# A written-out instruction order, priced anew, and one store moved to another queue, in a hybrid encoder block

## The chip, the core and the metric

The kernel runs on one core of a Trainium2 chip. A core has five engines with an instruction stream each: PE (TensorE, the matmuls, with PEld as its weight load), DVE (VectorE), ACT (ScalarE), POOL (GpSimd) and SP (SyncE, here only an issuer of DMAs). The metric is the device time of one execution in microseconds; less is better. The kernel before was timed in three runs.

## What is computed

One layer with width 1024 over 2048 tokens, in float32:

```python
hn = rmsnorm(h, mix_norm_g)
u, g_ssm, q, k, v, g_attn = split(hn @ w_in)            # six times 512 columns
y_ssm = s5_branch(u, ...) * silu(g_ssm)                 # diagonal complex state space, GELU, GLU
y_att = stick_breaking_branch(q, k, v, ...) * silu(g_attn)   # 8 heads of 64, strictly causal
h = h + concat(y_ssm, y_att) @ w_out
h = h + sigmoid(rmsnorm(h) @ w_ple_gate) * (p @ w_ple_proj)
...
# stick-breaking, for each block of 128 queries:
z = q @ k.T / 8
later = reverse_cumsum(log_sigmoid(-z)) - log_sigmoid(-z)
weights = exp(log_sigmoid(z) + later)                   # strictly below the diagonal
out = weights @ v
```

## The kernel before, in words

**Stages.** The work goes through five stages, which overlap.

1. `phase_u` (L547): eight units T of 256 tokens. `load_x` (L551) loads x, normalizes it, transposes it on PE in 64-row pieces (L527), splits it into a rounded part and a rest (`split`, L512) and stores it for later (hn, L565). Then u is projected with three matmuls for each product (L542 to L544: high by high, high by rest, rest by high). ACT copies the four results into the tile `uq` (L589), and at each odd T a DMA stores `uq` into the DRAM scratch tensor u, 1 MB at a time: four DMAs (L592), issued by POOL.
2. `ssm_chain` (L171) makes the state space's tables on DVE, beside stage 1.
3. `ssm_pack`, `ssm_batch` and `gate_unit`, eight batches of four state-space groups. Each batch loads its u for all tokens (`us`, L387), so the first needs all four stores of u. Matmuls L358, L364, L407, L467 to L470 and scans on DVE; POOL takes some products. `gate_unit` (L596) projects the gate.
4. Attention. Head pairs hp = 0 to 3, each with 16 blocks of 128 queries; block i of pair hp stands in step t = i + 8 hp, so up to two pairs run side by side. `attn_proj` (L662) projects q, k, v and the gate (L657 to L659, 128x512, three matmuls for each product; transposes L690, L691). `attn_block` (L701) goes through the keys in chunks of up to 512. For each chunk and both heads: z on PE, two heads abreast on 64 rows each (L718, six matmuls); ACT makes two sigmoids, px (L723) and be (L728); POOL masks the diagonal (L732); DVE runs a reverse scan of px (L734); POOL multiplies be by it (L736); PE transposes the weights in 64-row pieces, two abreast (L527, into ps_wt); ACT or DVE copies them out (L745, L743). For every two chunks the products with v follow (L753, two heads abreast on 64 columns each). The GLU of the state-space branch (`glu_unit`, L634) is mixed into the last eight steps.
5. `phase_out` (L829): 16 blocks of 128 rows, w_out (L657 to L659 into ps_h) and the gated embedding (into ps_p and ps_g).

**PSUM.** Eight banks are named z0, z1, w0, w1, tr, ssm, acc and o. z and the weights' transposes use two each for one chunk (z0 and z1, w0 and w1).

**Tilings.** PE uses the whole array for projections, half the rows for z and the 64-row transposes, and half the columns for the products with v. In the planner these are the modes "all", "rows" and "cols".

**What sets the order.** The order within each engine is not the order of the program text. When the program is written, `arrange` (L1293) lays out one order for each engine and adds it as dependencies. `plan` (L1077) lists for each instruction what it must wait for, its engine, and a length from `duration` (L1049), with the mode of each matmul. `list_schedule` (L1188) then runs a model: at each step it takes the engine that is free first and gives it the ready instruction of the best rank. Instructions ready are kept apart by mode; one of the present mode may be taken although another's rank is better by up to `near` (4 us); a change of mode costs a flat `change` (0.2 us). A DMA holds the modelled link for its bytes at 290 GB/s, behind 1.5 us and ahead of 2 us. `best_order` (L1260) does this six times, forward and then backward over reversed dependencies; the backward times give the next forward ranks, and the order with the earliest modelled end is kept. Groups written inside `abreast` (the pairs on half arrays) stay together.

An order, once laid out, is fixed: an engine whose next instruction has to wait does not take a later one. SP issues its DMAs in such an order too.

Of the kernel before, what the change touches and what calls it, by code (L numbers as in the profile page):

```python
# [18 lines left out]
P = 128  # L19
# [527 lines left out]
def phase_u(e, pool, xp, chain):  # L547
# [26 lines left out]
    for T in range(NT // 2):  # L574
        if 2 <= T + 1 < NT // 2:
            xts[T + 1] = load_x(T + 1)
        xt = xts.pop(T - 2, None)
        xt = xts[T]
        if T % 2 == 0:
            uq = pool.tile([P, L, 4, NCH // 4], F32, tag="uq", name="uq", bufs=2)  # L580
        ps = [e.bank("ps_u", "w0", "w1", "o", "acc")[:, :256] for _ in range(4)]
        if T == 2:
            e.mark()
        for ct, c in [(ct, c) for c in range(NC8) for ct in range(4)] if T == 0 else [(ct, c) for ct in range(4) for c in range(NC8)]:
            cs = slice(ct * P, (ct + 1) * P)
            mm3(e, ps[ct], (w[c][:, 0, cs], w[c][:, 1, cs]), (xt[:, :, 0, c], xt[:, :, 1, c]), c == 0, c == NC8 - 1)
        for ct in range(4):
            k0 = (T % 2) * (NCH // 8)
            nc.scalar.activation(uq[:, :, ct, k0:k0 + NCH // 8], ps[ct].rearrange("p (c j) -> p j c", j=L), AF.Copy)  # L589
        if T % 2 == 1:  # L590
            c0 = (T // 2) * (NCH // 4)
            nc.gpsimd.dma_start(e.u_d[:, :, c0:c0 + NCH // 4].rearrange("j (k p) c -> p (j k) c", p=P), uq.rearrange("p j k c -> p (j k) c"))  # L592
    return prep, xts


# [453 lines left out]
def duration(i, name, outs, ins, psum):  # L1049

    n = max([a[1] for a in outs + ins] or [1])
    eng = str(i.engine).split(".")[-1]
    if name == "InstDMACopy":
        return (0.6 if eng == "Pool" else 0.45), 0.0
    if name == "InstMatmult":
        cols, kind = outs[0][1], ins[0][2]
        if i.is_transpose:
            return (0.031 if ins[0][0] <= 64 else 0.109), 0.12
        if "float32r" in kind or "bfloat16" in kind:
            return {512: 0.228, 256: 0.120}.get(cols, max(cols / 2255.0, 0.058)) / (2 if ins[0][0] <= 64 else 1), 0.12  # L1060
        half = min(outs[0][0], ins[0][0]) <= 64
        return (1 if half else 2) * max(cols / 1160.0, 0.056), 0.12
    if eng == "Activation":
        return 0.193 + n * 0.00082, 0.0
    if eng == "Pool":
        if name == "InstTensorTensor" and "pow" in str(i.op).lower():
            return 0.45 + 0.15 * n, 0.0
        base, slope = {"InstMemset": (0.1, 0.0008), "InstTensorCopy": (0.5, 0.001), "InstTensorScalarPtr": (0.3, 0.001), "InstTensorScalarAffineSelect": (0.35, 0.0008)}.get(name, (0.47, 0.00175))
        return base + slope * n, 0.0
    if name == "InstTensorScalarPtr" and i.is_tensor_tensor_scan:  # L1070
        return 0.22 + n * 0.0027, 0.0
    if name in ("InstMemset", "InstTensorCopy") and not psum:
        return 0.11 + n * 0.0006, 0.0
    return 0.15 + n * 0.00107, 0.0


def plan(tc, pools):  # L1077
# [27 lines left out]
    for k, i in enumerate(mybir_i):  # L1105
# [79 lines left out]
    return _seen[key]  # L1185


def list_schedule(ops, pre, soft, length, mode, rank, near=4.0, change=0.2):  # L1188

    import heapq  # L1190
    n = len(ops)
# [3 lines left out]
    for k in range(n):  # L1195
        for q in (*pre[k], *soft[k]):
            after[q].append(k)
    for e in set(eng):
        free[e], wait[e], ready[e], order[e], now[e] = 0.0, [], {}, [], None

# [9 lines left out]
    for k in range(n):  # L1210
        if not open_[k]:
            heapq.heappush(wait[eng[k]], (0.0, rank[k], k))
    for _ in range(n):
        best = None
        for e in free:
            while wait[e] and wait[e][0][0] <= free[e]:
                _, r, k = heapq.heappop(wait[e])
                heapq.heappush(ready[e].setdefault(mode.get(k), []), (r, k))
            if any(ready[e].values()):
                c = (free[e], 0, e)  # L1220
            elif wait[e]:
# [6 lines left out]
        if late:  # L1228
            k = heapq.heappop(wait[e])[2]
        else:  # L1230
            m = min((h for h in ready[e] if ready[e][h]), key=lambda h: ready[e][h][0][0] - near * (h == now[e]))
            k = heapq.heappop(ready[e][m])[1]
        t = max(t, due(k))
        if now[e] != mode.get(k):
            t += change
            now[e] = mode.get(k)
        start[k] = t
        free[e] = t + length[k][0]
        if length[k][2]:
            link = max(t + 1.5, link) + length[k][2] / 290e3  # L1240
            done[k] = link + 2.0
# [18 lines left out]
def best_order(ops, pre, soft, length, mode, rows, turns=6):  # L1260
# [23 lines left out]
    for _ in range(turns):  # L1284
        order, start, done = list_schedule(ops, pre, soft, length, mode, lead([k - 1e5 if k in soon else r for k, r in enumerate(rank)], first))
        if best is None or max(done) < best[0]:
            best = max(done), order, start
        _, _, done = list_schedule(ops, back, loose, length, mode, lead([-t for t in done], last))
        rank = [-t for t in done]
    return best  # L1290

# [37 lines left out]
```

## Time and profile before

| What | us |
|---|---|
| median of three runs (1605.31 to 1606.29) | 1605.36 |
| profiled execution | 1606.73 |
| its span, first to last instruction | 1604.8 |
| PEld busy | 1254.5 |
| DVE busy | 1079.1 |
| ACT busy | 825.2 |
| POOL busy | 766.3 |

The difference between span and execution is 1.9 us around the instructions. Instruction counts and busy shares stand in the page's first part. The three matmuls of attn_proj are the largest group on PE, with 480 instructions to a line. The page's groups name the line, the engine, what is written from what, shapes, count, busy time, the mean of one in ns, and the idle time ahead of them with what ended it. The chain of waits follows the work that ended last back to the start. The table of windows gives each engine's busy time in a stretch of the span. The timeline gives starts and durations in order. A matmul's duration runs to its modelled end, and successive matmuls overlap: for the rate at which PE goes on, one looks at the difference of two starts.

### The profile page before, as it was taken

To read this page: it belongs to the slowest core of one execution; us is meant where nothing else is said; L and a number is where in the kernel's file an instruction comes from. 1 tells how busy PE (TensorE), PEld (TensorE's weight loads), DVE (VectorE), ACT (ScalarE), POOL (GpSimd) and SP (SyncE) were. 2 spreads that over 40 slices of the span, in tenths; PEclk is the share of its full clock that TensorE was granted. 3 is DMA by queue.
4 is the path that set the end of the run, shared out by engine and by line. 5 is a ranking of instruction groups with operands and counts; after the bars stand their busy time and mean duration, and the time that the engine had idled before them with its cause. 6 is when DMAs were issued, how large, how long until landed. Compare 5 with 4: busy or idle time off the path is not lost.

```text
span 1604.8 us, 31108 instructions
## 1 busy us (share of the span) xinstructions
PE 1548.5 (96%) x11878; PEld 1254.5 (78%) x11878; DVE 1079.1 (67%) x1980; ACT 825.2 (51%) x1850; POOL 766.3 (48%) x882
## 2 busy tenths in 40 slices
PE   6999898999999999999999999999989999999998
PEld 6998888987777777777777776777678788888887
DVE  6895948868678997789987899748764432332322
ACT  6643435456566776677766777646544221121211
POOL 2242434437578898688967798747630000000000
PEclk9999999999999999999999999999999999999999
DMA  9897535455332323323233234432354221212210
GB/s 294 262 289 194 175 118 181 156 174 193 113 113 84 112 91 132 113 85 108 95 132 112 86 109 112 109 96 68 107 164 126 83 79 50 86 60 69 64 49 33
DMA packets 147670, 195.58 MB, mean 122 GB/s; under 512 B 63697, under 2 KB 110753, under 8 KB 136129
## 3 DMA queue, kind: packets, MB, share of 16 engines
q1 hardware_dynamic: 145552, 186.45, 36.1%
q0 software_dynamic: 1968, 7.15, 2.2%
q8 instruction: 94, 1.54, 0.4%
q14 instruction: 56, 0.45, 0.1%
HBM read 145.44 MB, written 48.12 MB: 121 GB/s over the span
## 4 chain that ended last, share of the span: by engine, by line
PE 79%; DVE 11%; issue 4%; POOL 3%; ACT 1%; DMA 1%; SPq 0%; POOLq 0%; DVEq 0%; ACTq 0%
PE ps_qk L657 7%; PE ps_qk L659 7%; PE ps_qk L658 7%; PE ps_o L753 6%; PE ps_z L718 5%; PE ps_wt L527 4%; PE ps_g L659 4%; PE ps_h L657 4%; PE ps_h L658 4%; PE ps_g L658 4%; PE ps_h L659 4%; PE ps_g L657 4%; DVE px L734 3%; POOL be L736 2%; PE ps_u L543 2%
## 5 line engine op out<-in xcount | busy, mean ns | idle before, releaser
L736 POOL TENSOR_TENSOR be<-be,px 128x512 f32<-128x512 f32 (+3 forms) x320 | 404.1, 1275 | 136.6 <-DVE px L734 51.0
L734 DVE TENSOR_TENSOR_SCAN px<-px 128x512 f32<-128x512 f32 (+3 forms) x320 | 424.6, 1338 | 52.6 <-ACT px L723 37.0
L723 ACT ACTIVATE px<-ps_z 128x512 f32<-128x512 f32 (+3 forms) x320 | 170.0, 539 | 78.8 <-PE ps_z L718 51.9
L657 PE MATMUL ps_qk<-w_w,xt 128*128 128x512 f32 x480 | 198.7, 414 | 1.2 <-DVE gn L60 1.2
L658 PE MATMUL ps_qk<-w_w,xt 128*128 128x512 f32 x480 | 195.4, 407 | 0.0
L659 PE MATMUL ps_qk<-w_w,xt 128*128 128x512 f32 x480 | 195.3, 407 | 0.0
L508 POOL TENSOR_TENSOR rs_h<-rs_h,mhalf 128x1 f32<-128x1 f32 x16 | 9.1, 572 | 381.8 <-DVE rs_h L67 381.8
L728 ACT ACTIVATE be<-ps_z 128x512 f32<-128x512 f32 (+3 forms) x320 | 170.4, 545 | 5.4 <-PE ps_wt L527 5.4
L745 ACT ACTIVATE ws<-ps_wt 128x512 f32<-128x512 f32 (+3 forms) x256 | 129.0, 540 | 79.3 <-PE ps_wt L527 78.5
L718 PE MATMUL ps_z<-k,q 64*128 64x512 f32 (+3 forms) x960 | 138.5, 392 | 2.4 <-ACT be L728 1.5
L753 PE MATMUL ps_o<-ws,v 128*64 128x128 f32 x2176 | 138.3, 278 | 0.0
L753 PEld LDWEIGHTS ps_o<-ws,v 128*64 128x64 f32 x2176 | 118.7, 138 | 22.2 <-issue 18.1
L527 PEld LDWEIGHTS ps_wt<-ident,be 64*128 64x128 f32 x2176 | 83.1, 138 | 51.6 <-issue 25.6
L657 PEld LDWEIGHTS ps_qk<-w_w,xt 128*128 128x128 f32 x480 | 90.2, 188 | 32.1 <-issue 11.9
L659 PEld LDWEIGHTS ps_qk<-w_w,xt 128*128 128x128 f32 x480 | 90.3, 188 | 24.2 <-issue 5.7
L658 PEld LDWEIGHTS ps_qk<-w_w,xt 128*128 128x128 f32 x480 | 90.5, 189 | 23.5 <-issue 5.8
L527 PE MATMUL ps_wt<-ident,be 64*128 64x64 f32 x2176 | 102.9, 229 | 5.8 <-POOL be L736 2.8
L514 ACT ACTIVATE yr<-yt 128x512 fp32r<-128x512 f32 x32 | 20.2, 632 | 162.7 <-PE ps_h L659 157.3
L657 PE MATMUL ps_h<-w_w,yr 128*128 128x512 f32 x256 | 100.7, 393 | 2.3 <-ACT yr L514 2.3
L659 PE MATMUL ps_g<-w_wg,hr 128*128 128x512 f32 x256 | 101.5, 397 | 0.0
L658 PE MATMUL ps_g<-w_wg,hr 128*128 128x512 f32 x256 | 101.1, 395 | 0.0
L658 PE MATMUL ps_h<-w_w,yr 128*128 128x512 f32 x256 | 100.6, 393 | 0.0
(378 smaller groups left out, 3608.5 us busy)
## 6 DMA issues: line engine op xcount, KB each, us to landing
xt<-hn SPq DMA_DIRECT2D x60, 1024.0 KB, 4.9
hn<-xt SPq DMA_DIRECT2D x16, 1024.0 KB, 9.5
wst<-in_w_in_dram SPq DMA_DIRECT2D x48, 256.0 KB, 5.3
xg<-hn SPq DMA_DIRECT2D x12, 1024.0 KB, 7.0
x<-in_x_dram SPq DMA_DIRECT2D x16, 512.0 KB, 7.0
out_dram<-o SPq DMA_DIRECT2D x32, 256.0 KB, 2.0
h<-in_x_dram SPq DMA_DIRECT2D x15, 512.0 KB, 4.3
u<-uq POOLq DMA_DIRECT2D x4, 1024.0 KB, 18.3
```

The lines of the kernel that those rows point to most:

```text
L527: e.nc.tensor.transpose(ps[h][:, 64 * k:64 * k + 64], v[r], e.ident[r, r])
L543: mm(out, wh, xl, start=False, stop=False)
L657: mm(out, xh, wh, start=first, stop=False)
L658: mm(out, xh, wl, start=False, stop=False)
L659: mm(out, xl, wh, start=False, stop=last)
L718: nc.tensor.matmul(z[:, :n], q[half[h], a], A.k[ch][half[h], b, :n], start=s == 0, stop=s == 2)
L723: nc.scalar.activation(px[:, :n], z[:, :n], AF.Sigmoid, scale=-(HD ** -0.5))
L728: nc.scalar.activation(be[:, :n], z[:, :n], AF.Sigmoid, scale=HD ** -0.5)
L734: nc.vector.tensor_tensor_scan(rv, rv, rv, initial=1.0 if carry[h] is None else carry[h], op0=ALU.mult, op1=ALU.bypass)
L736: nc.gpsimd.tensor_tensor(be[:, :n], be[:, :n], px[:, 1:n + 1], op=ALU.mult)
L745: nc.scalar.activation(dst, ps, AF.Copy)
L753: nc.tensor.matmul(po[half[h], :P], A.v[sb][:, h], w[:, h, b], start=sb == i, stop=sb == 0)
```

## The change

One line of the kernel's own work is touched: the four stores of u are issued by SP and not by POOL. The rest is in the planner:

- `duration`: a DMA issued by POOL takes 0.6 us plus 0.27 ns for each piece (contiguous run of elements, counted by the new `pieces`). POOL's general instructions have base 0.2 us and not 0.47, its diagonal masks 0.25 and not 0.35; DVE's scan is 0.2 + 0.002 n and not 0.22 + 0.0027 n (n elements a partition).
- `plan`: on the link a piece counts for at least 220 bytes. DVE and POOL instructions that touch no PSUM get the mode "shared". The 64-row transposes get the mode "turn", which stands with "rows" when ready instructions are chosen, and apart from it when a change is priced.
- `list_schedule`: `near` is 8 us. A change costs what the new function `change` says, by the mode left and the one entered. With `stay` = 0.3 us: where the choice would leave the present mode, and an instruction of the present mode will be ready within 0.3 us with a rank at most `near` behind, the engine idles until then. A "shared" instruction that begins while the other engine of DVE and POOL is in one is lengthened by 0.45 of the overlap, or of its own length plus 0.2 us if that is less. In backward passes the change is priced with the two modes exchanged.

```diff
-            nc.gpsimd.dma_start(e.u_d[:, :, c0:c0 + NCH // 4].rearrange("j (k p) c -> p (j k) c", p=P), uq.rearrange("p j k c -> p (j k) c"))
+            nc.sync.dma_start(e.u_d[:, :, c0:c0 + NCH // 4].rearrange("j (k p) c -> p (j k) c", p=P), uq.rearrange("p j k c -> p (j k) c"))
...
-        return (0.6 if eng == "Pool" else 0.45), 0.0
+        return (0.6 + pieces(i) * 0.00027 if eng == "Pool" else 0.45), 0.0
...
-        base, slope = {"InstMemset": (0.1, 0.0008), "InstTensorCopy": (0.5, 0.001), "InstTensorScalarPtr": (0.3, 0.001), "InstTensorScalarAffineSelect": (0.35, 0.0008)}.get(name, (0.47, 0.00175))
+        base, slope = {"InstMemset": (0.1, 0.0008), "InstTensorCopy": (0.5, 0.001), "InstTensorScalarPtr": (0.3, 0.001), "InstTensorScalarAffineSelect": (0.25, 0.0008)}.get(name, (0.2, 0.00175))
...
-        return 0.22 + n * 0.0027, 0.0
+        return 0.2 + n * 0.002, 0.0
...
-        length.append(duration(i, type(i).__name__, outs, ins, psum) + ((outs[0][0] * outs[0][1] * 4 if type(i).__name__ == "InstDMACopy" else 0),))
+        length.append(duration(i, type(i).__name__, outs, ins, psum) + ((max(outs[0][0] * outs[0][1] * 4, pieces(i) * 220) if type(i).__name__ == "InstDMACopy" else 0),))
+        if not psum and str(i.engine).split(".")[-1] in ("DVE", "Pool") and type(i).__name__ not in ("InstDMACopy", "InstRegisterMove"):
+            mode[k] = "shared"
         if type(i).__name__ == "InstMatmult":
-            mode[k] = "rows" if ins[0][0] <= 64 else "cols" if outs[0][0] <= 64 else "all"
+            mode[k] = ("turn" if i.is_transpose else "rows") if ins[0][0] <= 64 else "cols" if outs[0][0] <= 64 else "all"
...
-def list_schedule(ops, pre, soft, length, mode, rank, near=4.0, change=0.2):
+def change(a, b):
+
+    if a == b or a is None or b is None or (a, b) == ("turn", "rows"):
+        return 0.0
+    if (a, b) == ("rows", "turn"):
+        return 0.09
+    return {"rows": 0.19, "turn": 0.12, "cols": 0.148, "all": 0.097}[a] + (0.1 if b == "all" else 0.0)
+
+
+def list_schedule(ops, pre, soft, length, mode, rank, near=8.0, stay=0.3, back=False):
...
             m = min((h for h in ready[e] if ready[e][h]), key=lambda h: ready[e][h][0][0] - near * (h == now[e]))
+            if m != now[e] and now[e] is not None:
+                r = ready[e][m][0][0]
+                soon = [w[0] for w in wait[e] if w[0] <= free[e] + stay and tiling.get(w[2]) == now[e] and w[1] - near <= r]
+                if soon:
+                    free[e] = min(soon)
+                    continue
...
-        if now[e] != mode.get(k):
-            t += change
-            now[e] = mode.get(k)
+        if k in tiling:
+            t += change(mode[k], last[e]) if back else change(last[e], mode[k])
+        now[e], last[e] = tiling.get(k), mode.get(k)
+        held = length[k][0]
+        if mode.get(k) == last.get(peer.get(e)) == "shared":
+            held += 0.45 * min(held + 0.2, max(0.0, free[peer[e]] - t))
...
-        free[e] = t + length[k][0]
+        free[e] = t + held
```

More of the change, by code (lines that the diff above doesn't have):

```diff
@@ L1074, in duration, with pieces @@
     return 0.15 + n * 0.00107, 0.0
+def pieces(i):
+    runs, total = [], 1
+    for side in (i.ins, i.outs):
+        run, total = 1, 1
+        ap = [(int(s), int(c)) for s, c in side[0].ap]
+        for s, c in reversed(ap):
+            if s == run:
+                run *= c
+            elif c > 1:
+                break
+        for _, c in ap:
+            total *= c
+        runs.append(run)
+    return total // min(runs)
 def plan(tc, pools):
@@ L1212, in list_schedule @@
             heapq.heappush(wait[eng[k]], (0.0, rank[k], k))
-    for _ in range(n):
+    left = n
+    while left:
         best = None
@@ L1217, in list_schedule @@
                 _, r, k = heapq.heappop(wait[e])
[L1218 removed]
+                heapq.heappush(ready[e].setdefault(tiling.get(k), []), (r, k))
             if any(ready[e].values()):
```

5 lines of the change are left out of this document (4 added, 1 removed).

## The prediction

> **What bounds the kernel now.** I read the page first: the busy shares, then the chain that ended last.
>
> ```profile
> span 1604.8 us, 31108 instructions
> PE 1548.5 (96%) x11878; PEld 1254.5 (78%) x11878; DVE 1079.1 (67%) x1980; ACT 825.2 (51%) x1850; POOL 766.3 (48%) x882
> PE 79%; DVE 11%; issue 4%; POOL 3%; ACT 1%; DMA 1%; SPq 0%; POOLq 0%; DVEq 0%; ACTq 0%
> ```
>
> TensorE is busy 96% of the span and holds 79% of the chain. A plan cannot change how many matmuls there are, so it can win time in two ways only: by leaving PE fewer idle stretches, or by making what counts as busy denser. The table by stretches says where either is to be had. Its columns are the stretch, its length, then busy time of PE, PEld, DVE, ACT, POOL, the granted clock, the DMA share and GB/s.
>
> ```profile
> 0.00:40.00 40.00, 25.57 (x234) 24.24 (x235) 25.98 (x99) 24.20 (x40) 11.71 (x24) 1.00 0.92 294
> 40.00:120.00 80.00, 78.65 (x744) 76.20 (x744) 69.36 (x248) 45.53 (x81) 28.36 (x19) 0.98 0.90 277
> 120.00:320.00 200.00, 183.42 (x1375) 177.32 (x1374) 143.80 (x235) 88.62 (x203) 74.57 (x39) 0.93 0.54 165
> 520.00:580.00 60.00, 59.09 (x602) 43.94 (x600) 56.39 (x91) 46.23 (x108) 50.78 (x59) 1.00 0.33 112
> 740.00:800.00 60.00, 58.82 (x598) 43.55 (x596) 56.59 (x91) 45.98 (x107) 57.83 (x62) 1.00 0.29 98
> 880.00:980.00 100.00, 97.99 (x976) 72.14 (x970) 90.83 (x145) 73.32 (x173) 86.76 (x97) 1.00 0.30 95
> 1120.00:1200.00 80.00, 71.64 (x548) 55.91 (x547) 56.82 (x72) 40.78 (x75) 42.36 (x40) 0.91 0.41 126
> 1200.00:1600.00 400.00, 397.99 (x1954) 323.25 (x1952) 134.72 (x217) 88.12 (x156) 9.14 (x16) 1.00 0.23 71
> ```
>
> Idle PE: 14.4 us while the first data come, 16.6 us in the state-space stage (120 to 320), 8.4 us where attention ends (1120 to 1200). In those last two the granted clock is 0.93 and 0.91. A clock of 0.93 over 200 us is worth up to 14 us, 0.91 over 80 us up to 7 us. The output stage from 1200 on has 2 us idle in 400: nothing to win. In the stretches of attention (345 to 1188) PE idles 1 to 2 us each, so there the density counts. In three of them, 220 us together, DVE is busy 56.39 + 56.59 + 90.83 = 203.8 us, 93%: DVE nearly binds too.
>
> What PE loses at a change of tiling is read from starts in the timeline (start, duration, engine, line, operation; x6 merges six); the two group rows behind it give the mean of one in ns.
>
> ```profile
> 400.73 0.38 PE L690 MATMUL ps_tq<-ident,qn 128*128 128x128 f32 x2
> 400.95 0.27 PE L691 MATMUL ps_tq<-ident,gn 128*128 128x128 f32 x1
> ...
> 402.68 0.40 PE L657 MATMUL ps_qk<-w_w,xt 128*128 128x512 f32 x1
> 403.00 0.96 PE L718 MATMUL ps_z<-k,q 64*128 64x512 f32 x6
> 403.90 0.33 PE L691 MATMUL ps_tq<-ident,gn 128*128 128x128 f32 x1
> 403.98 0.48 PE L658 MATMUL ps_qk<-w_w,xt 128*128 128x512 f32 x1
> 404.30 0.39 PE L659 MATMUL ps_qk<-w_w,xt 128*128 128x512 f32 x1
> 404.53 0.39 PE L657 MATMUL ps_qk<-w_w,xt 128*128 128x512 f32 x1
> ...
> 408.95 0.40 PE L658 MATMUL ps_qk<-w_w,xt 128*128 128x512 f32 x1
> 409.28 0.71 PE L527 MATMUL ps_wt<-ident,be 64*128 64x64 f32 x16
> 409.92 0.50 PE L659 MATMUL ps_qk<-w_w,xt 128*128 128x512 f32 x1
> 410.26 0.40 PE L657 MATMUL ps_qk<-w_w,xt 128*128 128x512 f32 x1
> ...
> 420.67 0.40 PE L658 MATMUL ps_qk<-w_w,xt 128*128 128x512 f32 x1
> 420.99 1.97 PE L753 MATMUL ps_o<-ws,v 128*64 128x128 f32 x32
> 422.89 0.50 PE L659 MATMUL ps_qk<-w_w,xt 128*128 128x512 f32 x1
> 423.23 0.40 PE L657 MATMUL ps_qk<-w_w,xt 128*128 128x512 f32 x1
> ```
>
> ```profile
> L753 PE MATMUL ps_o<-ws,v 128*64 128x128 f32 x2176 | 138.3, 278 | 0.0
> L527 PE MATMUL ps_wt<-ident,be 64*128 64x64 f32 x2176 | 102.9, 229 | 5.8 <-POOL be L736 2.8 <-ACT ws L745 2.5 <-DVE ws L743 0.5
> ```
>
> Undisturbed, a 512-column projection starts 0.23 us after the last (404.53 less 404.30). Three pairs of z, two abreast on half the rows each, should take 0.23 a pair, 0.69. From 402.68 to 404.30 are 1.62 us: less two projections (0.46), z (0.69) and L691 (0.11, the 0.38 of two L690 less the 0.27 of one), **0.36 us** are lost for entering and leaving. The transposes of weights: 410.26 less 408.95 is 1.31; less 0.46, and less 0.71 without the 0.23 that one lasts, which leaves 0.37 (0.30 if an eighth step of 0.07 is added). The output products: 423.23 less 420.67 is 2.56; less 0.46, and less 1.97 without 0.28, leaves 0.41 (0.30 with a sixteenth step of 0.11). So each interruption of the full-array stream costs about **0.35 us**, whatever interrupts it.
>
> How many are there? Walking along PE's matmuls in order, between these two (the first and the last change of the attention stage) I count 505 changes.
>
> ```profile
> 344.96 0.72 PE L718 MATMUL ps_z<-k,q 64*128 64x128 f32 x7 [0.93 <-DVE sg L60]
> ...
> 1185.86 1.97 PE L753 MATMUL ps_o<-ws,v 128*64 128x128 f32 x32
> 1187.76 0.50 PE L658 MATMUL ps_h<-w_w,yr 128*128 128x512 f32 x1
> ```
>
> 194 of them begin a full-array run: 194 x 0.35 is 68 us, the way in and the way out. The other 117 go between the small tilings (out of z into products, say); at 0.15 us, a little under half of 0.35, they cost 18. Together **86 us**, 5% of the span, and the stage's true bound. Transposes followed by z, 91 times, keep the same rows and I count them free.
>
> **The change, part by part.**
>
> *Prices and waiting.* The planner's flat 0.2 us per change becomes 0.19, 0.12, 0.148 or 0.097 us by the tiling that is left, plus 0.1 into the full array: in and out 0.387, 0.317, 0.345 us, beside some 0.35 above. The old price, 0.4 for in and out, was wrong by little in sum; the prices alone should move little. What moves the order is `near` from 4 to 8 us, so that PE leaves its tiling only for work that is more than 8 us more urgent in rank, and `stay`, an idle of at most 0.3 us in the plan if work of the present tiling is about to be ready. Idling 0.3 to save 0.35 is worth 0.05 a time at the least; joining is the gain. The bound: 160 groups of z and 161 runs of weight transposes; 121 of them already stand side by side (91 + 30). If the other 38 or so pairs met, that saves 38 x 0.35 = 13 us. There are 81 runs of output products with 162 ends; 87 of the ends touch a small tiling already. Were the 75 others to do so, each would spare about 0.2 us: 15 us. Ceiling 28 us; floor zero, or below it, since a longer run in one tiling makes a z group late (rival below). A group's z and its transposes stand a scan and a product apart, so most cannot meet: I take a third of the ceiling, **-9.5 us**.
>
> *Costs of DVE and POOL.* The rows:
>
> ```profile
> L736 POOL TENSOR_TENSOR be<-be,px 128x512 f32<-128x512 f32 (+3 forms) x320 | 404.1, 1275 | 136.6 <-DVE px L734 51.0
> L734 DVE TENSOR_TENSOR_SCAN px<-px 128x512 f32<-128x512 f32 (+3 forms) x320 | 424.6, 1338 | 52.6 <-ACT px L723 37.0
> ```
>
> For 512 columns the plan had 1.37 us (POOL) and 1.60 (scan), and gets 1.10 and 1.22, plus 45% of the overlap when both run. Means over all widths are 1.275 and 1.338, so for the scan the old price is too long and the new one plus some overlap is nearer. No instruction changes; only what the planner believes of the 203.8 us above. It may let it close part of the 8.4 us of idle at 1120 and of the 16.6 us at 120, or open as much. Bounds -15 and +15; I take **0**, because nothing in the rows tells the sign.
>
> *u by the sync queue.* Rows from the issues, waits, the timeline and the chain:
>
> ```profile
> u<-uq POOLq DMA_DIRECT2D x4, 1024.0 KB, 18.3
> out_dram<-o SPq DMA_DIRECT2D x32, 256.0 KB, 2.0
> zt<-z SPq DMA_DIRECT2D x16, 256.0 KB, 3.5
> ...
> PE ps_b L407 <- DMA us<-u: 3.5, 1, 3.5
> ...
> 128.26 2.81 POOL L592 DMA_DIRECT2D u<-uq  x1 [2.23 <-ACT uq L589]
> ...
> 142.74 3.92 DMA us<-u
> ```
>
> Four stores of 1 MB, each in 8192 pieces of 128 bytes; POOL is held 2.81 us for each and the last lands 14.4 us after it begins (142.7 less 128.3). SP moves pieces of the same size for zt: 2048 of them land in 3.5 us, where the like amount in large pieces lands in 2.0. Four times the 1.5 us between is 6 us, with the 2.0 about 8: u would land some **6 us earlier**. POOL's 4 x 2.81 = 11 us were beside an otherwise idle POOL and are worth nothing. The gain is the 3.5 us for which PE waits at the first L407, plus some of the slow clock after it: at most 5 us. What is late next is the rest of the state-space chain, which the loss of 16.6 us shows to be elsewhere too. I take **-4 us**. Costing pieces in the plan's link (220 bytes each, so u counts 1.8 MB) only tells the planner of this; it is in that number. On SP, u waits for ACT's copies, and x loads and hn stores stand behind it: rival two.
>
> The Trainium skill, "DMA: Bandwidth & Descriptors", section "Queues, rings and completion order", says that each DMA engine goes round its queue rows packet by packet, while one issuer's row is consumed in ring order. By that u on its own row shares bandwidth with the loads, and on SP's row it stands ahead of them: the rule speaks against this edit, and by it u's gain is rival two's. No run here has yet shown it for u.
>
> *Sum.* -9.5 - 4 = -13.5 us. The profiled execution took 1606.7 us with its span of 1604.8; the median of the three runs is 1605.4. Span 1591.3, time **1592 us** by the median.
>
> **The rivals.**
>
> *One: the longer stay starves DVE* (slower). Place: the 220 us where DVE is 93% busy, 16 us free. There are about 42 z groups there (160 over 843 us). PE held up to 4 us longer in projections delays a z group, with only two z banks, so DVE cannot take the next scan instead. If that leaves DVE idle 0.9 us more for each group, 38 us are added, of which 16 fit the slack: +22 us, less 9.5 and 4 gained gives **1614**. It decides from about 0.7 us a group (16 + 13.5 over 42). For it: DVE holds 11% of the chain. Against it: 0.9 us a group is what a plan with right prices of DVE would see.
>
> *Two: u stands ahead of the x loads.* 40 to 120 us has a DMA share of 0.90, and three of the four u stores fall there, each about 6 us of ring time. If half of 3 x 6 us reaches PE, +9 eats the 9.5 saved: **1605**. Against: PE idles only 1.35 us there, so loads come early.
>
> *Three: it doesn't do what it says.* Pairs that could meet already do, the count stays near 505, and only u remains: **1601**.
>
> *Four: the better prices also fill the holes.* Half of the idle 25 us and of the 21 us of slow clock at 120 to 320 and 1120 to 1200 would give -23 with u's 4 in it, and -9.5: **1573**.
>
> **How the numbers follow.** Forecast 1592 (1584 to 1599) 0.38; rival four 0.17; three 0.09; two 0.08; one 0.28. Faster by over 0.2% (3.2 us, about what a measurement of this kernel can tell from no change): 0.38 + 0.17 + 0.09 = 0.64; same 0.08; slower 0.28. The range reaches to rival four's and most of one's: 1573 to 1615, about 0.82. The likeliest sign's own range is 1573 to 1601.
>
> **What would show it.** Right: 505 changes fall to about 475, PE's busy time by some 10 us, attention ends that much before 1188; u's rows stand on SP, landing in about 8 us, and L407's wait on us is gone. Wrong: the count unchanged; DVE's idle before L734 well above 52.6 us; x loads landing far over their present time with PE waiting before 120 us; new idle and a lower clock at 120 to 320 or 1120 to 1200.

## The result, and the profile after

The changed kernel takes 1606.55 us (median of 14 runs, 1604.03 to 1608.25), the kernel before 1605.93 on the same chip (14 runs, 1603.56 to 1607.59): ratio 1.0005, interval 0.9997 to 1.0013. No difference can be measured, where 13.5 us less were forecast. The profiled execution took 1608.2 us.

First the page of the changed kernel: span, busy shares, chain, two groups and two DMA issues.

```profile
span 1606.4 us, 31085 instructions
PE 1545.0 (96%) x11878; PEld 1265.4 (79%) x11878; DVE 1067.4 (66%) x1980; ACT 820.9 (51%) x1850; POOL 750.2 (47%) x878
PE 83%; DVE 6%; POOL 4%; issue 3%; ACT 2%; DMA 1%; SPq 0%; POOLq 0%; DVEq 0%; ACTq 0%
...
L736 POOL TENSOR_TENSOR be<-be,px 128x512 f32<-128x512 f32 (+3 forms) x320 | 417.6, 1318 | 124.0 <-DVE px L734 36.6
L734 DVE TENSOR_TENSOR_SCAN px<-px 128x512 f32<-128x512 f32 (+3 forms) x320 | 413.7, 1305 | 61.7 <-ACT px L723 35.8
...
x<-in_x_dram SPq DMA_DIRECT2D x16, 512.0 KB, 8.3
...
u<-uq SPq DMA_DIRECT2D x4, 1024.0 KB, 8.8
```

PE's busy time fell by 3.5 us (1548.5 before) and the span grew by 1.6: PE stands idle 61.4 us of it, and 56.3 before. DVE's share of the chain went from 11% to 6% and PE's from 79% to 83%, so nothing here points at DVE as a new bound. u lands in 8.8 us and not 18.3.

Then the table by stretches (columns as in the prediction), the changed kernel's first:

```profile
0.00:40.00 40.00, 26.95 (x245) 25.44 (x246) 26.56 (x102) 24.71 (x41) 11.95 (x23) 1.00 0.80 266
40.00:120.00 80.00, 75.37 (x713) 72.61 (x712) 64.54 (x248) 44.43 (x80) 17.24 (x15) 0.98 0.94 290
120.00:320.00 200.00, 186.76 (x1396) 180.75 (x1395) 140.13 (x230) 87.81 (x202) 70.52 (x38) 0.92 0.54 165
345.00:1120.00 775.00, 763.03 (x6808) 584.11 (x6809) 626.67 (x1081) 522.27 (x1268) 592.94 (x744) 0.99 0.35 113
...
740.00:800.00 60.00, 57.48 (x553) 44.68 (x554) 57.11 (x89) 42.94 (x99) 55.18 (x62) 0.97 0.28 93
880.00:980.00 100.00, 95.83 (x952) 71.23 (x952) 89.39 (x144) 73.89 (x174) 86.08 (x100) 1.00 0.25 86
1120.00:1200.00 80.00, 71.60 (x586) 56.97 (x585) 56.59 (x71) 42.36 (x77) 44.60 (x41) 0.94 0.42 124
1200.00:1600.00 400.00, 396.25 (x1939) 321.51 (x1938) 133.06 (x215) 84.43 (x153) 8.22 (x15) 1.00 0.22 71
```

and of the kernel before the one stretch that the prediction did not show:

```profile
345.00:1120.00 775.00, 767.31 (x6834) 574.32 (x6835) 628.20 (x1077) 523.93 (x1270) 596.20 (x744) 1.00 0.35 112
```

In attention (345 to 1120) PE idles 12.0 us and not 7.7, and its clock is 0.99 and not 1.00. From 880 to 980 it idles 4.2 us where it idled 2.0. The early stretch from 40 to 120 idles 4.6 and not 1.35.

**Where the time went.** I walked along PE's matmuls. From each difference of two starts I took what a matmul of that shape takes when undisturbed, and the price of a change of tiling as the diff has it. What is left is called idle where PE's modelled end lies before the next start, slow where the stretch had half the clock, and other else. The undisturbed work is 1418.3 us in both kernels. (Stages end at the last ps_u, the first z, the last product ps_o and the end of the span, some 4.7 us behind PE's last matmul. The walk counts from the first instruction, which stands at 0.3 us in the timelines, so its times are 0.3 us smaller than theirs. All in us, before / after.)

| Stage | ends at | changes | idle | slow clock | other |
|---|---|---|---|---|---|
| start (first matmul at 10.8 / 7.4) | 126.1 / 129.3 | 4.7 / 4.3 | 5.7 / 11.7 | 1.5 / 1.5 | 3.0 / 3.2 |
| state space | 344.7 / 345.6 | 0.1 / 0.1 | 19.5 / 17.0 | 11.8 / 13.0 | 0.3 / 0.2 |
| attention | 1187.2 / 1189.2 | **85.7 / 72.1** | 20.4 / 26.3 | 5.8 / 8.8 | 8.1 / 9.6 |
| output | 1604.5 / 1606.1 | 5.3 / 5.3 | 2.0 / 4.0 | 0 / 1.5 | -3.3 / -3.3 |

So the forecast saving is there by the diff's prices, and larger than forecast: the 505 changes of attention became 451, which is 13.5 us. But attention and output give back 5.9 + 3.0 + 1.5 + 2.0 + 1.5 = 13.9 us as idle PE, slow clock and loose ends, and the gain by u is nowhere to be seen: the first z comes at 345.6 and came at 344.7. The experiments had to say who takes each back.

### The profile page after: what moved, and what is told of

The parts are those of the page before. It is cut to its first block, busy times and chain, and to the rows that moved or that the text cites. A ratio compares the mean times of both kernels' runs of the same rounds, so it can differ in the third digit from the quotient of the medians.

```text
span 1606.4 us, 31085 instructions
## 1 busy us (share of the span) xinstructions
PE 1545.0 (96%) x11878; PEld 1265.4 (79%) x11878; DVE 1067.4 (66%) x1980; ACT 820.9 (51%) x1850; POOL 750.2 (47%) x878
## 3 DMA queue, kind: packets, MB, share of 16 engines
q8 instruction: 94, 1.54, 0.4%
## 4 chain that ended last, share of the span: by engine, by line
PE 83%; DVE 6%; POOL 4%; issue 3%; ACT 2%; DMA 1%; SPq 0%; POOLq 0%; DVEq 0%; ACTq 0%
PE ps_qk L657 7%; PE ps_qk L658 7%; PE ps_qk L659 7%; PE ps_o L753 6%; PE ps_z L718 6%; PE ps_wt L527 4%; PE ps_g L657 4%; PE ps_h L657 4%; PE ps_g L659 4%; PE ps_g L658 4%; PE ps_h L658 4%; PE ps_h L659 4%; POOL be L736 2%; PE ps_u L543 2%; PE ps_u L542 2%
## 5 line engine op out<-in xcount | busy, mean ns | idle before, releaser
L736 POOL TENSOR_TENSOR be<-be,px 128x512 f32<-128x512 f32 (+3 forms) x320 | 417.6, 1318 | 124.0 <-DVE px L734 36.6
L734 DVE TENSOR_TENSOR_SCAN px<-px 128x512 f32<-128x512 f32 (+3 forms) x320 | 413.7, 1305 | 61.7 <-ACT px L723 35.8
L527 PEld LDWEIGHTS ps_wt<-ident,be 64*128 64x128 f32 x2176 | 86.9, 139 | 48.5 <-issue 22.6
L718 PEld LDWEIGHTS ps_z<-k,q 64*128 64x128 f32 x960 | 78.7, 188 | 31.8 <-issue 16.9
L508 POOL TENSOR_TENSOR rs_qk<-rs_qk,mhalf 128x4 f32<-128x4 f32 x64 | 77.4, 1210 | 50.1 <-DVE rs_qk L67 49.1
L657 PE MATMUL ps_h<-w_w,yr 128*128 128x512 f32 x256 | 100.2, 391 | 0.0
```

The lines of the kernel that those rows point to most:

```text
L508: nc.gpsimd.tensor_tensor(r, r, e.mhalf[:, :n], op=ALU.pow)
L527: e.nc.tensor.transpose(ps[h][:, 64 * k:64 * k + 64], v[r], e.ident[r, r])
L657: mm(out, xh, wh, start=first, stop=False)
L718: nc.tensor.matmul(z[:, :n], q[half[h], a], A.k[ch][half[h], b, :n], start=s == 0, stop=s == 2)
L734: nc.vector.tensor_tensor_scan(rv, rv, rv, initial=1.0 if carry[h] is None else carry[h], op0=ALU.mult, op1=ALU.bypass)
L736: nc.gpsimd.tensor_tensor(be[:, :n], be[:, :n], px[:, 1:n + 1], op=ALU.mult)
```

## The experiments

Two theories were put against each other at first. The first: DVE and POOL hold PE back as the plan now orders them (rival one). The second: the order as a whole gives back what it saves, through PE's idle and its clock, whatever DVE's speed. Later runs set other rivals against the second, as their expectations say. Several kernels lay an order down from a stored list in place of the planner's call:

```diff
-    ops, pre, *rest = plan(tc, pools)
-    _, order, _ = best_order(ops, pre, *rest, rows)
+    ops = list(tc.nc.cur_bb.bb.instructions)
+    order = stored(ORDER)
```

Each median stands beside that of the kernel before on the same chip.

**One part alone, and the change without it.** e1 keeps before's order on every engine and moves only the four u stores to SP; e2 keeps the changed order and issues u from POOL:

```diff
-            nc.gpsimd.dma_start(e.u_d[:, :, c0:c0 + NCH // 4] ...
+            nc.sync.dma_start(e.u_d[:, :, c0:c0 + NCH // 4] ...
```

> The kernel before with its own order on every engine, laid down as it was, and only the four stores of u moved from POOL to SP, at the places in SP's order where the plan of before starts them. First theory (u on SP is a gain, and the new order loses it again): the wait of 3.5 us of the first L407 on us goes, u lands in 9 us or less, the time falls by 3 to 5 us, to about 1601. Second theory (u ahead of the x loads on SP's queue costs what it gains): within 1 us of the kernel before, with PE idle before 120 us grown by 3 us or more.

> The changed kernel with its own order on every engine, and only the four stores of u put back on POOL, at the places where the plan of after starts them. First theory (u on SP is a gain): slower than the changed kernel by 3 to 5 us, about 1610, with a wait on us back near 140 us. Second theory (u on SP costs early): within 1 us or faster than the changed kernel, with PE idle before 120 us smaller than the 11.7 us counted in the changed kernel.

e1: 1599.09 beside 1606.33, ratio 0.9959 (0.9945 to 0.9972). e2: 1609.53 beside 1606.33, ratio 1.0021 (1.0013 to 1.003). So u on SP is worth 7.2 us by itself (by the interval, 4.5 to 8.8) and about 3 us in the changed order (e2's interval just touches the changed kernel's); the rest of the change makes the kernel some 3 us slower. The wait on us that e2's expectation named did not come back: PE waits nowhere for us there, so those 3 us come from elsewhere, and from where is open. The timeline of e1, at the first product with us and at the first z:

```profile
143.38 0.82 PE L407 MATMUL ps_b<-us,stB 128*128 128x128 f32 x5 [0.54 <-DMA us<-u]
...
337.70 0.72 PE L718 MATMUL ps_z<-k,q 64*128 64x128 f32 x7 [0.93 <-DVE sg L60]
```

and of the changed kernel:

```profile
151.44 0.28 PE L544 MATMUL ps_sg<-xt,w_w 128*128 128x256 f32 x1
151.56 0.28 PE L542 MATMUL ps_sg<-xt,w_w 128*128 128x256 f32 x1
151.68 0.49 PE L407 MATMUL ps_b<-us,stB 128*128 128x128 f32 x3
...
345.94 0.72 PE L718 MATMUL ps_z<-k,q 64*128 64x128 f32 x7 [0.93 <-DVE sg L60]
```

In e1 L407 stands at 143.4 (146.7 before, behind a wait of 3.5), and the first z at 337.7 (344.96 before): 3.3 us became 7.3 on the way through the state-space stage, since that stage's slow clock fell from 11.8 to 7.9 us and its idle from 19.5 to 16.5. In the changed kernel u is on SP too, no wait is left ahead of L407, and yet it stands 8.3 us later than in e1. Ahead of it PE runs 64 gate products (ps_sg) from 143.9 on, 0.12 us from start to start with no idle between: it is PE's own order that puts L407 behind them. (e1's profiled execution, 1595.8 us, is the fastest of its five and 3.3 us under their median; its worth goes by the median.)

**Less work for DVE and POOL, in both orders.** The scan and the product behind it do half their columns (so half of the cumulative product is left out):

```diff
+            rv = rv[:, :n // 2]
-            nc.gpsimd.tensor_tensor(be[:, :n], be[:, :n], px[:, 1:n + 1], op=ALU.mult)
+            nc.gpsimd.tensor_tensor(be[:, :n // 2], be[:, :n // 2], px[:, 1:n // 2 + 1], op=ALU.mult)
```

> The kernel before with its own order, and the reverse scan on DVE and the product on POOL (L734, L736) done on the first half of their columns only, so half of the attention's cumulative product is left out. First theory (in attention the order of PE waits for DVE and POOL): PE's idle time in attention, 12.8 us here before, falls below 5 us and the time by 8 us or more. Second theory (idle PE comes from elsewhere): it stays above 10 us and the time within 4 us.

> The changed kernel with its own order, and the same halved scan and product as in the run before it. First theory (the 13.9 us saved at changes of tiling are handed back because PE, now ahead, waits for DVE and POOL): with the two made light PE no longer waits in attention, the slow clock there (13.6 us of it) goes, and this kernel is 8 to 14 us faster than the light version of the kernel before. Second theory (what is handed back is elsewhere or is nothing but the order's luck with other waits): it is within 4 us of the light version of the kernel before.

e3: 1586.06 beside 1606.33, ratio 0.9874 (0.986 to 0.9887). e4: 1588.93, ratio 0.9886 (0.9873 to 0.99). The scan's group in e3, then in e4:

```profile
L735 DVE TENSOR_TENSOR_SCAN px<-px 128x256 f32<-128x256 f32 (+3 forms) x320 | 224.4, 711 | 97.8 <-ACT px L723 79.6 <-POOL px L732 17.0
```

```profile
L735 DVE TENSOR_TENSOR_SCAN px<-px 128x256 f32<-128x256 f32 (+3 forms) x320 | 224.8, 711 | 102.8 <-ACT px L723 78.2 <-POOL px L732 19.0 <-POOL px L725 3.6
```

The scan's 414 to 425 us became 224, and both orders gain about the same: 20.3 us from before's 1606.3, some 18 from the changed kernel's 1606.6. So PE does wait for DVE and POOL in attention: by the walk, the idle there falls from 20.4 to 5.6 us with before's order, and from 26.3 to 11.9 with the changed one. But were the longer stay starving DVE, the changed order would gain more by lighter DVE work, and it doesn't. That is against the first theory. The idle that the new order adds (6.3 us in the light versions, and 5.9 at full work) is not DVE's or POOL's speed.

**The sizes `near` and `stay`.** One number changed in `list_schedule` each time: e5 is the changed kernel with near 4, e14 with stay 0.15, and e6 the kernel before with near 8.

```diff
-def list_schedule(ops, pre, soft, length, mode, rank, near=4.0, change=0.2):
+def list_schedule(ops, pre, soft, length, mode, rank, near=8.0, change=0.2):
```

> The changed kernel with near back at 4 us; the prices, stay, the costs and u on SP stay. The planner counts 542 changes of tiling instead of 505 in its own instructions. First theory (near of 8 buys fewer changes with idle PE in attention, and the two cancel): changes cost some 5 us more by their prices, idle PE and slow clock in attention (19.8 and 5.6 us in the changed kernel) fall by 3 to 8 us, and the time is 0 to 4 us below the changed kernel. Second theory (fewer changes are a clear gain, and what is lost is lost outside attention): 4 to 6 us above the changed kernel, about 1611.

> The kernel before with near at 8 us and nothing else changed: the flat price of 0.2 us, no stay, the old costs of DVE and POOL, u on POOL. First theory (near of 8 buys fewer changes with idle PE): changes fall by about 20, worth 5 us, but PE idles some 15 us more in attention, with slow clock behind it, and the time is 8 to 20 us above the kernel before. Second theory (a longer stay is good by itself): 3 to 8 us below the kernel before.

> The changed kernel with stay 0.15 and not 0.3 us, a small step that the planner's model holds for nothing (its own end moves by 1 us). First theory (what the plan gives beyond its model is the luck of each order: which waits of a microsecond or two arise, and how they meet the clock): the time differs from the changed kernel by more than 3 us, either way, and the first z moves by more than 5 us. Second theory (the measured times follow the model): within 3 us of the changed kernel, 1604 to 1609.

e5: 1611.14 beside 1606.87, ratio 1.0026 (1.0017 to 1.0036). e6: 1628.18, ratio 1.0134 (1.0118 to 1.0151). e14: 1607.55 beside 1606.11, ratio 1.0008 (0.9999 to 1.0018). The first 120 us of e6, then of the kernel before:

```profile
0.00:120.00 120.00, 95.40 (x890) 91.53 (x890) 92.42 (x340) 65.81 (x115) 38.62 (x42) 0.97 0.86 265
```

```profile
0.00:120.00 120.00, 104.22 (x976) 100.44 (x977) 95.35 (x346) 69.73 (x121) 40.07 (x42) 0.99 0.91 283
```

With the old prices a longer stay costs 21.3 us. In these 120 us PE does 86 matmuls fewer, and the last ps_u comes at 139.3 (126.1 before): the walk has 12.1 us more idle in the start. In attention it saves 4.9 us of changes (85.7 to 80.8) and pays with 7.2 us of idle (20.4 to 27.6). That is the trade in its bare form: fewer changes bought with idle PE; but most of the 21.3 us is the start's. Going back to near 4 in the changed kernel (e5) gains nothing either: it is 4.3 us behind the kernel before, and its first z stands at 351.1 (345.9 in the changed kernel). In attention the trade runs backward there: 483 changes cost 4.8 us more than the changed kernel's 451, and some 7 us of idle and slow clock go; the loss is ahead of attention. (The 542 and 505 of e5's expectation are the planner's own counts over all stages.) So near isn't by itself what makes the changed order no better. Halving `stay` moves nothing that can be told from the changed kernel, so nothing says that the short wait is what costs.

**Which stage's order.** The four that follow splice orders, all with u on SP. e7 has before's order for the first 125 us of the plan's time (the last ps_u) and lets the changed planner do the rest. e8 is the same with near 4 and stay 0. e9 is e7 up to the first z and before's order from there. e10 is the changed kernel's order for the first 125 us and before's order behind it.

> All instructions that the kernel before begins in its first 125 us by the model keep the order of before (with u on SP); the rest is laid out by the changed planner as it is (near 8, stay 0.3). First theory (the changed order loses in three places: 2.6 us in the first 120 us, 3.8 us in the state-space stage, and in attention as much as it saves): 2 to 6 us below the changed kernel, 1601 to 1604, above the run that has only u moved (1599). Second theory (the first 120 us do not matter, since PE is full behind them): within 1.5 us of the changed kernel.

> As the run before it, but the rest laid out with near 4 and stay 0, and so with the new prices and costs alone. By the planner's own model PE idles 12.9 us in attention here, 22.6 in the changed kernel and 15.8 in the kernel before, while changes cost 89 us, 81 in the changed kernel and 96 in the kernel before. First theory (the new prices and costs are right and near and stay are what hands the gain back): below the run with only u moved, 1585 to 1596. Second theory (any new order loses to the old one by luck in waits the model doesn't see): 1599 to 1607.

> The order of the run with before's start and the changed plan (1593.4 us) up to the first z of the model, and behind it the order of the kernel before (u on SP). So it differs from that run in the order of attention and output alone. First theory (in attention and output the new order hands back all of the 13.5 us that it saves at changes, and some more): first z stays near 330 us, from there to the end 1256 to 1260 us, the time 1586 to 1592. Second theory (the new order of attention is a gain that only the start hides): 5 us or more above that run, 1598 or more.

> The changed kernel's order for all that it begins in its first 125 us by the model, and behind it the order of the kernel before (u on SP). Beside the run with only u moved (1599) it has another start alone. First theory (the changed start itself delays the first product with u by some 8 us, as the trace has it, and all behind it): 1603 to 1609, the first L407 at 147 to 152 us instead of 143. Second theory (the start costs only its 2 to 3 us, and the state-space order behind it the rest): 1600 to 1602.

| Kernel | start | state space | attention, output | us | before | ratio (interval) |
|---|---|---|---|---|---|---|
| e1 | old | old | old | 1599.09 | 1606.33 | 0.9959 (0.9945 to 0.9972) |
| e10 | new | old | old | 1601.40 | 1606.28 | 0.9974 (0.9965 to 0.9982) |
| after | new | new | new | 1606.55 | 1605.93 | 1.0005 (0.9997 to 1.0013) |
| e9 | old | replanned | old | 1592.47 | 1606.28 | 0.992 (0.9907 to 0.9933) |
| e7 | old | replanned | replanned | 1593.42 | 1606.87 | 0.9921 (0.9908 to 0.9934) |
| e8 | old | replanned, near 4 | replanned, near 4 | 1594.23 | 1606.87 | 0.9924 (0.9911 to 0.9938) |

This is the table that decides. **The attention order is worth nothing**: e7 and e9 differ in it alone (with the output's), and by 1 us, well inside their intervals. With 505 changes in attention (e9), 492 (e8) and 451 (e7) the kernel takes 1592.5, 1594.2 and 1593.4 us: the number of changes doesn't set the time. The walk for that pair (e9 to e7, from the first z): changes -13.5, idle in attention +5.8, slow clock there +7.0, other +0.5, idle in the output stage +2.1: together +1.9, and z to the end takes 1260.7 us and not 1259.0.

**The state-space order is worth 6.6 us** behind before's start (1599.1 to 1592.5), which no term of the prediction's sum had. **The start costs some 2.3 us** (1599.1 to 1601.4; the two intervals overlap, so its size is uncertain), and the new state-space and attention orders behind it cost another 5.2. No run has the new start and the new state space with the old attention, so that the attention order is worth nothing behind that start too rests on the walk's table above.

e9 and e7 beat both kernels, by 13 us. e8, as fast as they are, has neither the longer stay nor the wait: what the new plan wins behind the old start it wins without them. Whether the new prices and costs win it, or any plan that knows that u is on SP, no run tells. By the walk, e9's state-space stage has 14.1 us of idle and 3.2 of slow clock where e1's has 16.5 and 7.9, and its first z comes 6.9 us earlier. The state-space stage in the changed kernel, then in e9:

```profile
120.00:345.00 225.00, 210.15 (x1593) 203.73 (x1591) 158.62 (x264) 102.14 (x231) 75.22 (x42) 0.93 0.52 159
```

```profile
120.00:345.00 225.00, 211.21 (x1649) 201.90 (x1650) 172.22 (x283) 111.57 (x257) 82.99 (x67) 0.98 0.57 175
```

```profile
143.77 1.45 PE L407 MATMUL ps_b<-us,stB 128*128 128x128 f32 x11
...
330.81 0.72 PE L718 MATMUL ps_z<-k,q 64*128 64x128 f32 x7 [0.93 <-DVE sg L60]
```

The timeline rows are e9's. PE is busy for the same time within 1.1 us, yet e9 gets its first z out 15.1 us earlier (330.8 and 345.9): the clock is 0.98 and not 0.93. By the walk, the stage from the last ps_u to z has 3.2 us of slow clock in e9 and 13.0 in the changed kernel, and 14.1 us of idle and not 17.0; and the last ps_u comes 3.3 us earlier (126.0 and 129.3). A busy share says nothing of this; the clock's column does.

**Is it the queue of u?** On SP each u store holds up the next DMA, as the changed kernel's SP queue shows:

```profile
75.16 0.38 SPq L592 DMA_DIRECT2D u<-uq  x1
77.41 7.37 SPq L487 DMA_DIRECT2D wst<-in_w_in_dram  x2
...
130.36 0.38 SPq L592 DMA_DIRECT2D u<-uq  x1
130.83 7.51 SPq L389 DMA_DIRECT2D tabs<-tb  x2
143.33 0.32 SPq L602 DMA_DIRECT2D xg<-hn  x1
143.70 0.94 SPq L387 DMA_DIRECT2D us<-u  x2
```

The third theory to be tried was that this hold, or the loads ahead of us behind it, makes L407 late. e11 is e9 and e12 the changed kernel with u issued by ACT behind its own copies; e13 is the changed kernel with the two us loads ahead of gs, lag and xg on SP.

```diff
-            nc.sync.dma_start(e.u_d[:, :, c0:c0 + NCH // 4] ...
+            nc.scalar.dma_start(e.u_d[:, :, c0:c0 + NCH // 4] ...
```

> As the run e9, with the four stores of u issued by ACT, each right behind the last copy into its uq, so that SP's queue holds no u. In all runs with u on SP the next issue on SP takes 6 to 8 us instead of 0.3 to 0.4; with u on POOL none does. First theory (the hold is on the issuer's own next DMA, and ACT has no other): no issue on SP above 3 us before 140 us, ACT is held only some 0.4 us for each u, u lands in 9 us or less, the time is 0 to 4 us below e9. Second theory (the hold is in ACT's own stream then, for what follows the DMA): ACT's next instruction is late by 6 us or more four times, and the time is 3 to 10 us above e9.

> The changed kernel with its own order, and only the four stores of u issued by ACT behind the last copy into uq. First theory (SP being held behind u, with us, tabs and x loads queued there, makes the changed kernel's start late): the first L407 comes 3 us or more before 151.4 us and the time is 3 to 8 us below the changed kernel, 1599 to 1603. Second theory (the order of the loads on SP, an xg load ahead of us among them, makes it late whoever issues u): within 2 us of the changed kernel.

> The changed kernel with its own order, except that on SP the first two loads of us stand ahead of the two stores of gs, the store of lag and the loads of xg that they followed. First theory (the xg load of 1 MB that the plan put ahead of us makes the first product with u, and the state-space stage behind it, late): the first L407 at 144 to 148 us instead of 151.4, the first z and the end 3 to 6 us earlier, 1600 to 1603. Second theory (the state-space stage is not held by its first product; its own waits and the slow clock behind them set its end): first L407 earlier, first z within 2 us of 345.6, the time within 2 us of the changed kernel.

e11: 1594.65 beside 1606.28, ratio 0.9931 (0.9918 to 0.9944). e12: 1607.28, ratio 1.001 (1.0001 to 1.0019). e13: 1609.07 beside 1606.11, ratio 1.0012 (1.0003 to 1.0021). In e11 ACT goes on at once, and so does SP:

```profile
127.00 0.39 ACT L589 ACTIVATE uq<-ps_u 128x256 f32<-128x256 f32 x1 [2.50 <-PE ps_u L544]
127.41 0.37 ACTq L592 DMA_DIRECT2D u<-uq  x1
127.88 0.60 ACT L359 ACTIVATE stB<-ps_pack 128x512 f32<-128x512 f32 x1 [0.50 <-PE ps_pack L358]
```

The hold is gone and no time is won, in either order; in e12 L407 stands at 153.1. e13 was a miss for both theories: its us loads are issued at 140.45 and not 143.70, and its first L407 still starts at 152.98, not earlier than in the changed kernel. So neither the hold nor the loads set L407's place. e10 shows that the order does: it has the changed start and before's order behind it, and L407 waits on us again, 4.5 us earlier than in the changed kernel.

```profile
147.20 1.09 PE L407 MATMUL ps_b<-us,stB 128*128 128x128 f32 x7 [2.62 <-DMA us<-u]
```

That within this order it is PE's part is argued from the timeline of PE ahead of L407, not shown by a run that moves L407 alone. And L407's place does not set the end of the stage: in e5 it comes 3.5 us earlier than in the changed kernel (148.2) and the first z 5.2 later, in e13 1.3 later and the first z 2.7 earlier (343.25).

## Why the prediction was wrong, point by point

**The sum, 13.5 us less: wrong by all of it.** The step that failed is the -9.5 us for prices and `stay`. The prediction called the price of the changes attention's "true bound", counted how many could go, and let each go at its full price with PE's idle left as it was. The count was even better than forecast (451, not 475; 13.5 us saved and not 9.5, by the diff's prices of 0.32 to 0.39 us in and out). But a matmul that is moved to join others of its tiling starts when its operands are ready, or makes something else late; e7 beside e9 gives the saving and its return in one pair: -13.5 and +15.4. The term should have stood at 0 (measured: e7 is 0.9 us slower than e9, within both intervals). The prediction had this return only as rival one, and put it on DVE. The whole miss is 14.1 us. It is made up of 9.5 that attention did not give and 7.5 for the new start and what was planned behind it, less 3.2 that u gave more than forecast (13.8 in sum).

**"Costs of DVE and POOL: 0, nothing tells the sign".** As a term that a replanned start and state-space stage can move either way it was the right warning with the wrong middle. Of the stretches that it named, 120 to 320 moved; 1120 to 1200 idles 8.4 us as before. The bounds of 15 held: the state-space order alone gives -6.6 us behind the one start, and the changed start with what was planned behind it takes 7.5 (1599.1 to 1606.55). Which of the planner's new numbers chose that start is open: with near 4 (e5) the last ps_u comes at 130.6, as late as in the changed kernel, so near alone isn't it; the prices of DVE, POOL and the link were not tried one by one. The prediction's reading of the rows was loose: its means of 1.338 and 1.275 us are over four widths, and it set them beside prices for 512 columns. Of 512 columns the scans take 1.54 us in the mean and the products 1.45 (224 each), near the old prices (1.60 and 1.37); the few that ran while the other engine did nothing (22 and 6, under 0.1 us of overlap) take 1.28 and 1.09, near the new ones (1.22 and 1.10). So the new prices were sound with their addition for overlap, and the rows shown did not say so.

**u by SP, -4 us: right in sign and mechanism, too small.** Alone it is -7.2 us, and 4.5 at the least by its interval, so the bound of 5 may or may not be broken. u lands in 9.7 us in e1 and 8.8 in the changed kernel, where some 8 were forecast, and the wait at L407 fell by 3.0 us of 3.5. The prediction priced the slow clock behind the wait at 1.5 us at most; in e1's profiled execution, its fastest, it gave about 4. In the changed kernel L407 stands behind gate products, so this wait is no part of what u gains there.

**The rivals.** *One* (a longer stay starves DVE): its trade, idle for changes, is real (in e6, 7.2 us of idle for 4.9 of changes in attention), but the cause was wrong: e3 and e4 show no more relief in the changed order than in before's, and DVE's idle ahead of the scan is 61.7 us, 9 more than before's 52.6. *Two* (u ahead of the x loads): wrong. In e1 the last ps_u stands at 125.8, before's at 126.1, with u on SP. x loads land in 8.3 us and not 7.0 in the changed kernel and PE idles 3.3 us more from 40 to 120, but e12 takes u off SP, its x loads land in 6.5, and it gains nothing. The Trainium skill, "DMA: Bandwidth & Descriptors", section "Queues, rings and completion order", whose rule of rings consumed in order stood behind this rival, is not contradicted: transfers behind u do start later. But in e1, where only u moved, PE idles 1.33 us from 40 to 120, and 1.35 before. *Three* (nothing but u remains) was right that attention yields nothing, for the wrong reason: the count did fall. *Four* (the holes get filled) came true in small part and only with before's start: 6.6 us in e9's state-space stage, where it asked for 19 beside u.

**What to see.** Of the signs for a right one, u's rows stand on SP and L407's wait is gone, but PE's busy time fell by 3.5 us and not 10, and the last product starts at 1189 (1187 before). Of the signs for a wrong one, DVE's idle and the x loads' landing grew as above. New idle came, but not at the places named: 3.3 us from 40 to 120 and 4.3 from 345 to 1120, while 120 to 320 idles 13.2 us and not 16.6, at a clock of 0.92 (0.93 before), and at 1120 to 1200 the idle stayed and the clock rose from 0.91 to 0.94.

## What to carry to other kernels

A saving counted on a bound engine is worth its price only where the next operands are ready that much earlier; count the idle that it opens beside it, stage by stage, before it goes into a sum. A change to a planner moves every stage: splice the old and new orders at stage borders, and the stage that pays and the one that costs fall apart (here u -7.2, the start +2.3, what follows that start +5.2, the attention order 0, behind a total of nothing). Where an engine's clock falls after short idle stretches, read the clock's column beside the busy share.

## What the runs showed of the hardware that was not expected

**Half clock after 1.4 us of idle.** The granted clock falls in whole stretches of 3.41 us on a fixed grid (half-clock stretches of both kernels last 3.41, 6.83 or 10.24 us). Three neighbouring stretches of the changed kernel in attention, and two near its end:

```profile
784.40:787.80 3.40, 3.40 (x53) 2.76 (x54) 2.50 (x4) 3.20 (x8) 3.37 (x8) 1.00 0.40 123
787.80:791.20 3.40, 2.00 (x28) 1.63 (x28) 3.40 (x4) 2.46 (x6) 2.17 (x4) 1.00 0.58 232
791.20:794.60 3.40, 3.05 (x32) 2.72 (x34) 3.37 (x7) 2.67 (x9) 3.40 (x4) 0.55 0.10 36
...
1088.20:1091.60 3.40, 2.38 (x11) 1.64 (x10) 3.23 (x7) 1.16 (x3) 1.71 (x2) 1.00 0.54 85
1091.60:1095.00 3.40, 3.40 (x48) 2.65 (x47) 2.07 (x4) 1.10 (x4) 0.47 (x2) 1.00 0.88 209
```

PE idles 1.40 us in the second and the next has half the clock (0.55, the borders not quite meeting); it idles 1.02 in the fourth and the next is full. In both kernels together, after the first 20 us, 19 of 20 full-clock stretches of the grid with 1.35 us of idle or more had a half-clock one behind them, and 0 of 10 with 0.9 to 1.32. In the other runs about one in seven of the stretches with 1.35 us or more had none behind it, the longest with 1.9 us, and a few with 1.28 to 1.34 had one, so the border is near 1.35 and not sharp. Half-clock stretches take 44 us before and 61 us in the changed kernel, outside the end; between 345 and 1120 none and 13.7. So idle of 1.4 us within one stretch can cost up to 1.7 us more (half of 3.41) in the next, and the same idle spread over two need not: the planner prices neither. The Trainium skill, "TensorE: Matmul & The Clock Gate", section "Part 1", has the window (about 3.4 us, free-running) as measured here; its advice in "Why this matters for your kernels", no idle gaps over about 3 us, is not enough here, where some 1.4 us did it.

**An issuer's own hold.** The SP issue that follows a u store of 8192 pieces takes 6.3 to 10.2 us in the runs with u on SP (7.37 and 7.51 above hold one such issue and a short one each); most other issues take under 0.5. ACT's next activation began 0.47 us after it issued the same store. u landed in 18.3 us from POOL (16.6 in e2), 8.8 from SP (9.7 in e1) and 10.4 from ACT in e11, but 15.8 in e12.
